# Two cross-attention heads stay on chip and their output share moves forward in a hybrid decoder trunk

## The chip, the cores and the metric

The kernel runs as one program on one core of a Trainium2 chip. The metric is the device time of one execution in microseconds (us), as the median of several runs. TensorE (PE) multiplies matrices; VectorE (DVE), ScalarE (ACT) and GpSimd (POOL) work on elements; SyncE (SP) issues the transfers between DRAM and on-chip memory.

## What is computed

One inference step of a trunk of two layers, for a prompt of 512 tokens and a sample group of 8 times 4 tokens that share all weights; both lie side by side as 544 columns. Layer 0 is a dilated attention. Layer 1, where all of the change lies, is an RWKV-7 layer with 12 heads of 64 and four heads of cross attention into 256 memory tokens. Cut to what matters (`p` is the input projection of the normalised `x`; the cross heads are the last 256 of the 1024 branch columns):

```python
y, S = wkv_scan(r, decay, k, v, -kk, kk * a, s0)
y = group_norm(y) * ln_w + ln_b + jnp.sum(r * k * r_k, axis=-1, keepdims=True) * v
o_mem = cross_attn(q_mem, mem_kv)
h = jnp.concatenate([y, o_mem], axis=-1) * jax.nn.silu(gate)
x = x + rms_norm(h @ w_out, norm_post)
```

## The kernel before

Everything is in float32. A float32 product is made on PE as three products of a high and a low part (lines 313, 314 and 315 in `mm1`: high by high, low weight by high, high weight by low input). Weights come by DMA as pieces of 128 x 512 and are split by ACT (line 305) and POOL (line 306).

Layer 1 works on rows of 128 features. There are 29 feature columns of the input projection (`column`: r, k, v and the low-rank inputs; `gate`: gates 0 to 7 and the two query columns of the cross heads), each of 8 x 2 x 3 matmuls of 272 columns. Six pairs of heads make three groups of four heads, g = 0, 1, 2. For each group there are, in this order: elementwise work on DVE (decay, keys, receptance, values), score matrices (`sc`, masked into SA and SR on DVE at line 1381), a triangular solve of 30 steps on DVE (two instructions for each step, lines 1450 and 1452, in tile T; TX is its transpose, line 1460), products on PE (X at line 1466, then w, q, v), and a recurrence over eight chunks (`recur`): PE makes z from the state St, DVE adds it to UV (line 1676), PE makes z from UV, DVE makes the next St (line 1694), and y goes to a group norm (`norm`, `normed`: sums, square on ACT, power on POOL line 1537, product yc on DVE line 1538, transposition gn on PE line 1547, and back into bv on DVE line 1558).

What sets the order: `Flow` runs Python generators, each with a rank, and picks at each step the ready one of lowest rank. A `yield a, b` books `a` us of PE work and makes the generator ready `b` us later; the table `LAT` holds such delays, `RANK` the ranks, and a dense generator (projection columns, gates, output) is let in when the `debt` of the others is over `DEBT`. So PE's order, and with it that of the other engines, is written out before the program runs. The dense generators fill PE between the dependent steps of the solve and the recurrence. `GORDER` is the order of the eight gate columns, and the first `GEARLY` of them may come before the last feature column.

The output projection is `outer`. A gate column leaves `u` = gate times (for gates 6 and 7) the cross heads' output `om`; `u` is written to DRAM (`ud`, line 1195). `gated(j)` reads it back (`ug`, line 1758), for heads 0 to 5 multiplies it with the group norm's `bv` (DVE, line 1762), and makes its high part `h` on ACT (line 1763) and its low part on POOL, or on DVE for the `j` in `LOD` (line 1764). The output has eight row tiles `mt` in two parts of the columns: part 0 is 256 wide and part 1 288. Three shares are summed in `z`: `o1b` (the cross heads 6 and 7; 16 tiles of 6 matmuls, copied to z by ACT, line 1866), `o1a` (heads 0 to 3; 16 tiles of 12 matmuls, added by DVE, line 1881), and, in `last`, `o2` (heads 4 and 5, weights w2h and w2l; added by DVE, line 1812). `o1b` waits for gates, for the end of group 1's recurrence (`end1`) and for two of its norms, since z lies in tiles (tags AR and BK) that group 1 has used.

`last(i)` then takes the squares of part i (ACT line 1815, summed on POOL line 1818 and by PE products with ones), their inverse root (`rstd_begin`, `rstd_mid`, `rstd_end`; power on POOL, line 341), and `finish` scales each row (DVE, line 1782), adds the residual (`xr`; POOL line 1788, or DVE line 1785 for the rows in `RADD`) and sends it out.

## Time and profile before

| | |
|---|---|
| median of 3 runs | 808.15 us (806.22 to 809.14) |
| the profiled execution | 807.1 us, span 805.3 us |
| PE busy | 746.5 us (93%) |
| DVE busy | 468.2 us (58%) |
| ACT, POOL busy | 340.9 us (42%), 351.9 us (44%) |
| the chain that ended last | PE 75%, DVE 12%, DMA 4%, POOL 3%, ACT 2% |
| mean granted clock of PE | 0.979 of full speed |

Times in the rows are microseconds from the start of the span. An engine's idle time in brackets stands before the instruction that ended it, with the instruction that it waited for. The granted clock is 1.00 at 2.4 GHz and 0.50 at 1.2 GHz. Tile names are the program's, without their numbers.

### The profile page before, as it was taken

To read this page: it belongs to the slowest core of one execution; us is meant where nothing else is said; L and a number is where in the kernel's file an instruction comes from. 1 tells how busy PE (TensorE), PEld (TensorE's weight loads), DVE (VectorE), ACT (ScalarE), POOL (GpSimd) and SP (SyncE) were. 2 spreads that over 40 slices of the span, in tenths; PEclk is the share of its full clock that TensorE was granted. 3 is DMA by queue.
4 is the path that set the end of the run, shared out by engine and by line. 5 is a ranking of instruction groups with operands and counts; after the bars stand their busy time and mean duration, and the time that the engine had idled before them with its cause. 6 is when DMAs were issued, how large, how long until landed. Compare 5 with 4: busy or idle time off the path is not lost.

```text
span 805.3 us, 20097 instructions
## 1 busy us (share of the span) xinstructions
PE 746.5 (93%) x8264; PEld 633.0 (79%) x8264; DVE 468.2 (58%) x1100; ACT 340.9 (42%) x787; POOL 351.9 (44%) x391
## 2 busy tenths in 40 slices
PE   6899999999988988989999999999999999799793
PEld 5777778889875776688988889898788988589673
DVE  7743312255467455663454579854699536983465
ACT  6455321134343345535786247432365332442031
POOL 3642223333220262964543347644365445463257
PEclk9999999999999999999999999999999999799996
DMA  7474398852213574325213442200222233442013
GB/s 247 124 239 141 101 285 298 279 209 82 81 54 94 212 226 144 109 89 178 68 65 93 144 148 73 74 28 28 70 70 95 81 110 98 127 129 64 31 39 111
DMA packets 59088, 99.51 MB, mean 124 GB/s; under 512 B 6415, under 2 KB 24111, under 8 KB 58959
## 3 DMA queue, kind: packets, MB, share of 16 engines
q1 hardware_dynamic: 58996, 98.22, 37.1%
q8 instruction: 65, 1.06, 0.5%
q14 instruction: 27, 0.22, 0.1%
HBM read 84.15 MB, written 14.05 MB: 122 GB/s over the span
## 4 chain that ended last, share of the span: by engine, by line
PE 75%; DVE 12%; DMA 4%; POOL 3%; ACT 2%; issue 2%; SPq 1%; POOLq 0%; ACTq 0%; DVEq 0%
PE o L313 2%; PE b_h L313 2%; PE b_h L314 2%; PE b_h L315 2%; PE o L315 2%; PE sc L1373 2%; PE o L314 2%; PE y L1636 2%; PE Sx L560 2%; PE o L777 1%; PE z L1636 1%; DMA raw_wo<-in_w_out_a 1%; PE ssz L987 1%; PE ox L584 1%; PE pa L769 1%
## 5 line engine op out<-in xcount | busy, mean ns | idle before, releaser
L306 POOL TENSOR_TENSOR lo_b<-raw_b,hi_b 128x512 fp32r<-128x512 f32 x58 | 76.6, 1320 | 117.3 <-ACT hi_b L305 83.7
L306 POOL TENSOR_TENSOR lo_a<-raw_a,hi_a 128x512 fp32r<-128x512 f32 x44 | 57.1, 1299 | 138.6 <-ACT hi_a L305 138.0
L305 ACT CAST hi_a<-raw_a 128x512 fp32r<-128x512 f32 x44 | 27.3, 620 | 67.8 <-DMA raw_a<-in_w_in_a 9.7
L305 ACT CAST hi_b<-raw_b 128x512 fp32r<-128x512 f32 x58 | 36.3, 626 | 41.8 <-PE b_h L315 14.1
L313 PE MATMUL b_h<-xg,hi_b 128*128 128x272 f32 x160 | 46.5, 299 | 0.6 <-DVE xv L1133 0.3
L314 PE MATMUL b_h<-xg,lo_b 128*128 128x272 f32 x160 | 45.9, 294 | 0.0
L315 PE MATMUL b_h<-xg,hi_b 128*128 128x272 f32 x160 | 45.4, 292 | 0.0
L1450 DVE TENSOR_TENSOR TX<-T,TT 128x30 f32<-128x30 f32 (+14 forms) x90 | 29.3, 326 | 5.8 <-ACT T L1424 4.1
L313 PEld LDWEIGHTS b_h<-xg,hi_b 128*128 128x128 f32 x160 | 29.6, 188 | 2.9 <-issue 1.8
L1452 DVE TENSOR_TENSOR T<-T,TX 128x30 f32<-128x30 f32 (+14 forms) x90 | 30.1, 334 | 2.3 <-DVE TX L1450 0.4
L314 PEld LDWEIGHTS b_h<-xg,lo_b 128*128 128x128 f32 x160 | 29.7, 188 | 0.3
L315 PEld LDWEIGHTS b_h<-xg,hi_b 128*128 128x128 f32 x160 | 29.7, 188 | 0.3 <-issue 0.2
L1678 POOL TENSOR_TENSOR Sd<-St,DF 128x128 f32<-128x128 f32 x21 | 8.4, 401 | 37.4 <-DVE St L1694 26.7
L754 ACT ACTIVATE P<-P,m 128x768 f32<-128x768 f32 x16 | 14.9, 935 | 16.3 <-DVE m L753 16.3
L1373 PE MATMUL sc<-AR,BK 64*64 64x128 f32 x384 | 19.0, 279 | 0.2 <-DVE bv L1319 0.2
L313 PE MATMUL o<-h,hi_o1a 128*128 128x256 f32 (+1 forms) x64 | 18.8, 299 | 0.0
L314 PE MATMUL o<-h,lo_o1a 128*128 128x256 f32 (+1 forms) x64 | 18.5, 291 | 0.0
L315 PE MATMUL o<-h,hi_o1a 128*128 128x256 f32 (+1 forms) x64 | 18.1, 290 | 0.0
L769 PE MATMUL pa<-ident,P 128*128 128x128 f32 x96 | 14.2, 279 | 3.6 <-DVE P L756 1.4
L769 PEld LDWEIGHTS pa<-ident,P 128*128 128x128 f32 x96 | 10.6, 142 | 6.7 <-issue 2.3
L306 POOL TENSOR_TENSOR lo_o1a<-raw_o1a,hi_o1a 128x512 fp32r<-128x512 f32 x8 | 10.6, 1325 | 11.8 <-ACT hi_o1a L305 11.8
L1282 POOL TENSOR_TENSOR rv<-rv,mhalf 128x10 f32<-128x10 f32 x6 | 14.0, 2334 | 3.7 <-DVE rv L1281 3.7
(1057 smaller groups left out, 2825.9 us busy)
## 6 DMA issues: line engine op xcount, KB each, us to landing
raw_b<-in_w_in_b SPq DMA_DIRECT2D x58, 256.0 KB, 2.6
raw_a<-in_w_in_a SPq DMA_DIRECT2D x44, 256.0 KB, 2.7
kc<-in_kc SPq DMA_DIRECT2D x18, 512.0 KB, 5.2
vc<-in_vc SPq DMA_DIRECT2D x18, 512.0 KB, 6.2
out_win<-t SPq DMA_DIRECT2D x12, 272.0 KB, 2.3
PB<-bd SPq DMA_DIRECT2D x4, 576.0 KB, 6.7
x<-in_x SPq DMA_DIRECT2D x8, 272.0 KB, 6.0
xr<-in_x SPq DMA_DIRECT2D x16, 136.0 KB, 4.3
```

Source lines behind the costliest of these rows:

```text
L305: nc.scalar.copy(hi, raw)
L306: lo_eng.tensor_tensor(lo, raw, hi.bitcast(F32), ALU.subtract)
L313: nc.tensor.matmul(ps[:, :n], hi, xh, start=first, stop=False)
L314: nc.tensor.matmul(ps[:, :n], lo, xh, start=False, stop=False)
L315: nc.tensor.matmul(ps[:, :n], hi, xl, start=False, stop=last)
L560: nc.tensor.matmul(S[hh][64 * e:64 * e + 64, 0:256], qm[r, f, a:a + 64], kT[l][r, f, :], start=True, stop=True)
L754: nc.scalar.activation(P, P, AF.Exp, bias=m1[:, 0:1], scale=1.0, accum_out=m1[:, 1:2])
L769: nc.tensor.transpose(dst, P[:, j * 128:j * 128 + 128], ident)
L1373: nc.tensor.matmul(pts[e][unit(c, j, h)[0], a:a + 128], BK[H2[h], j, x, CH[c]], AR[H2[h], j, :, CH[c]], start=True, stop=True)
L1450: nc.vector.tensor_tensor(pd, TP[:, 0:s, s:s + 1].to_broadcast([128, s, w]), TT[:, s:s + 1, s + 1:32].to_broadcast([128, s, w]), ALU.mult)
L1452: nc.vector.tensor_tensor(TP[:, 0:s, s + 1:32], TP[:, 0:s, s + 1:32], pd, ALU.add)
L1636: nc.tensor.matmul(out, lhs, rhs, start=start, stop=stop)
```

## The change

Gates 6 and 7 no longer go through DRAM. When such a gate's half is made, its high part is copied by ACT and its low part subtracted (DVE for 6, POOL for 7) into tiles `hx` that take four of the six `tmp` buffers. For those buffers the gate waits until the last group's values are made (`values5`). A new generator `crossed` makes the sixteen `o1b` tiles right behind the last gate column. Its z rows lie in five column tiles, two `tmp` tiles and one row of the later squares' tile, so only the last row waits for `end1`. `outer` begins with the `o1a` share. The squares get tiles of their own. In the last part the residual adds are dealt out anew: DVE takes rows 6 and 7 of part 0 and rows 2 and 7 of part 1, POOL the other twelve. The first three adds of part 0 stand behind the squares' sums, two more rows of part 0 are scaled ahead of `rstd_begin`, and POOL's order there is fixed by hand as DVE's was. Seven constants of the planner are new.

```diff
-GORDER = (6, 2, 5, 4, 0, 1, 7, 3)
+GORDER = (4, 0, 5, 7, 2, 6, 3, 1)
-RADD = (0,)
+RADD = (6, 7), (2, 7)
+MID = 2
-GEARLY = 2
-LAT = [4.0, 5.82, 0.81, 0.26, 5.42, 5.2, 1.5, 0.94, 1.83, 0.6, 0.87]
-RANK = [3.5, 2, 4, 3, 2, 2.5, 2.5, 9]
-RHO, DEBT = 0.35, 0.5
-LOD = (1, 3)
+GEARLY = 5
+LAT = [4.0, 4.95, 0.81, 0.26, 5.42, 2.6, 1.5, 0.9, 1.56, 0.61, 1.28]
+RANK = [5, 7, 7, 3, 2, 2.5, 2.5, 9]
+RHO, DEBT = 0.35, 0.54
+LOD = (6, 0, 2)
...
             if j >= 6:
                 nc.vector.tensor_tensor(s, s, oj[:, HALF[h]], ALU.mult)
+                nc.scalar.copy(hx[j][0][:, HALF[h]], s)
+                (nc.vector if j in LOD else nc.gpsimd).tensor_tensor(hx[j][1][:, HALF[h]], s, hx[j][0][:, HALF[h]].bitcast(F32), ALU.subtract)
+        if 6 <= j < 8:
+            hx[j] = [pp.tile([128, NT], F32R, tag="tmp", bufs=TMPB, name=f"h{j}{k}") for k in range(2)]
...
-        if j < 8:
+        if j < 6:
             nc.sync.dma_start(ud[j], uj)
+        elif j < 8 and len(hx) == 2:
+            flow.done("hx", 1.5)
...
+            if j in (6, 7):
+                yield "values5"
             yield from gate(j)
...
+        for kt in range(len(FIN)):
+            residual(0, kt, out.xr)
+        for _ in range(MID):
+            finish(0, rp0, left.pop(0), out.xr, False)
         rv = rstd_begin(acc, n, "p11", 4e-6)
...
+    def crossed():
+        yield "columns"
+        yield "hx"
+        zt = [col(f"z1{mt}") for mt in range(5)]
+        zt += [tmp(f"z1{mt}") for mt in (5, 6)]
+        for mt in range(8):
+            if mt == 7:
+                yield "end1"
+                out.sq = [rw.tile([128, 2176], F32, tag=("AR", "BK")[i], bufs=2, name=f"sq1{i}") for i in range(2)]
+                zt.append(out.sq[0][:, 0:NT])
...
     def outer():
         yield "gates"
         out.h1 = pxg.tile([128, 2, 8, NT], F32R, tag="xg", name="h1")
-        for j in (6, 7):
-            gated(j)
-            yield 0.0, 1.0
-        for e in ("end1", "norm1_8", "norm1s"):
+        yield "crossed"
+        for e in ("norm1_8", "norm1s"):
             yield e
-        out.z = [by_row(i, ("AR", "BK")[i], 2176, "z1")[1] for i in range(2)]
+        for m in range(4):
+            gated(m)
...
+    flow.spawn(9.5, crossed(), True)
```

**Where the instructions go.** Up to about 400 us every engine's order is the same. PE's matmuls are the same in number and shape over the whole program, and also over the stretch up to the first `o1a` tile.

On PE, where the output share begins: in the kernel before the last gate column ends some rows earlier, transposes of the last group (`bk5s`) stand before it, and the first two tiles o000 and o001 (row tile 0, parts 0 and 1) interleave their halves for heads 6 and 7.

```order
L1362 MATMUL bk5s_8511<-ident_75,BK2_7065 32x64 x4
L313 MATMUL o000_9546<-h1_9492,hi_o1b0_9537 128x256
L314 MATMUL o000_9546<-h1_9492,lo_o1b0_9538 128x256
L313 MATMUL o001_9585<-h1_9492,hi_o1b0_9537 128x288
L314 MATMUL o001_9585<-h1_9492,lo_o1b0_9538 128x288
L315 MATMUL o000_9546<-h1_9492,hi_o1b0_9537 128x256
L315 MATMUL o001_9585<-h1_9492,hi_o1b0_9537 128x288
L313 MATMUL o000_9546<-h1_9492,hi_o1b0_9537 128x256
L314 MATMUL o000_9546<-h1_9492,lo_o1b0_9538 128x256
L313 MATMUL o001_9585<-h1_9492,hi_o1b0_9537 128x288
L314 MATMUL o001_9585<-h1_9492,lo_o1b0_9538 128x288
L315 MATMUL o000_9546<-h1_9492,hi_o1b0_9537 128x256
```

In the changed kernel the last gate column (`b11`) stands directly before the tiles, and the operands are `h60` to `h71`, made by the gates themselves.

```order
L314 MATMUL b11_h1_9222<-xg1_3424,hi_b11_1_9217 128x272
L315 MATMUL b11_h1_9222<-xg1_3424,lo_b11_1_9218 128x272
L316 MATMUL b11_h1_9222<-xg1_3424,hi_b11_1_9217 128x272
L314 MATMUL o000_9532<-h60_8811,hi_o1b0_9528 128x256
L315 MATMUL o000_9532<-h60_8811,lo_o1b0_9529 128x256
L316 MATMUL o000_9532<-h61_8812,hi_o1b0_9528 128x256
L314 MATMUL o000_9532<-h70_8618,hi_o1b0_9528 128x256
L315 MATMUL o000_9532<-h70_8618,lo_o1b0_9529 128x256
L316 MATMUL o000_9532<-h71_8619,hi_o1b0_9528 128x256
L314 MATMUL o001_9542<-h60_8811,hi_o1b0_9528 128x288
```

What moved: the 16 tiles are the same 96 matmuls, now behind 43 matmuls of gate columns (before 17) since the end of group 1's recurrence, and without the tile `h1` that was read back from DRAM.

On PE, in the recurrence of the last group (z2 and y2, with its states St2_0 to St2_7): before, tiles of the heads' share (o170, o171) stand between the steps, 50 matmuls between the first z and the fourth step.

```order
L315 MATMUL o170_10037<-h1_9492,hi_o1a7_10033 128x256
L313 MATMUL o170_10037<-h1_9492,hi_o1a7_10033 128x256
L314 MATMUL o170_10037<-h1_9492,lo_o1a7_10034 128x256
L315 MATMUL o170_10037<-h1_9492,hi_o1a7_10033 128x256
L1636 MATMUL z2_9188<-St2_2_9308,AR2_7064 64x64 x4
L1636 MATMUL y2_0_9228<-St2_1_9267,AR2_7064 64x64 x2
L1636 MATMUL y2_0_9228<-St2_2_9308,AR2_7064 64x64 x2
L313 MATMUL o171_10051<-h1_9492,hi_o1a7_10033 128x288
L314 MATMUL o171_10051<-h1_9492,lo_o1a7_10034 128x288
```

In the changed kernel nothing but the sample group's small products stands between the steps.

```order
L1645 MATMUL z2_9164<-St2_1_9259,AR2_6998 64x64 x4
L1645 MATMUL y2_0_9204<-UV2_7477,SR2_7476 64x64 x8
L1645 MATMUL y2_0_9204<-St2_0_9173,AR2_6998 64x64 x2
L1645 MATMUL y2_0_9204<-UV2_7477,SR2_7476 64x64 x8
L1645 MATMUL z2_9164<-UV2_7477,BK2_6999 64x64 x8
L1645 MATMUL z2_9164<-St2_2_9300,AR2_6998 64x64 x4
L1645 MATMUL y2_0_9204<-St2_1_9259,AR2_6998 64x64 x2
L1645 MATMUL y2_0_9204<-St2_2_9300,AR2_6998 64x64 x2
L1645 MATMUL z2_9164<-UV2_7477,BK2_6999 64x64 x8
L1645 MATMUL z2_9164<-St2_3_9344,AR2_6998 64x64 x4
```

What moved: the heads' share. Twelve of its 16 tiles stand ahead of the last group's first solve product X, six before; the other four stand between X and w, and none is left behind w. Ten of DVE's adds for these tiles then stand ahead of the transposition TX, four before. In the same way, the transposition norm `gn` of the last chunks (gn2_6) stands behind the first two `o2` tiles; before it stood behind the first four.

On POOL, at the end of the program (L1818/L1840 squares, L1788/L1808 residual adds, rv_p11 the power of part 1): before, two adds of part 0 stand among the squares and twelve adds behind the power.

```order
L1818 TENSOR_TENSOR sqo101_10194<-sqo101_10194,sqo141_10243 128x288
L1788 TENSOR_TENSOR z10_9530<-z10_9530,xr10_10065 128x256
L1818 TENSOR_TENSOR sqo101_10194<-sqo101_10194,sqo151_10254 128x288
L1788 TENSOR_TENSOR z10_9530<-z10_9530,xr10_10065 128x256
L341 TENSOR_TENSOR rv_p11_10292<-rv_p11_10292,mhalf_80 128x3
L1788 TENSOR_TENSOR z10_9530<-z10_9530,xr10_10065 128x256 x5
L1788 TENSOR_TENSOR z11_9531<-z11_9531,xr11_10175 128x288 x6
L1788 TENSOR_TENSOR z17_9532<-z17_9532,xr17_10176 128x288
```

In the changed kernel three stand behind the squares and nine behind the power: three of part 0 and six of part 1.

```order
L1840 TENSOR_TENSOR sq11_9745<-sq11_9745 128x288 x5
L1808 TENSOR_TENSOR z10_9519<-z10_9519,xr10_10073 128x256
L1808 TENSOR_TENSOR z11_9520<-z11_9520,xr10_10073 128x256
L1808 TENSOR_TENSOR z12_9521<-z12_9521,xr10_10073 128x256
L342 TENSOR_TENSOR rv_p11_10286<-rv_p11_10286,mhalf_80 128x3
L1808 TENSOR_TENSOR z13_9522<-z13_9522,xr10_10073 128x256
L1808 TENSOR_TENSOR z14_9523<-z14_9523,xr10_10073 128x256
L1808 TENSOR_TENSOR z15_9524<-z15_9524,xr10_10073 128x256
L1808 TENSOR_TENSOR z10_9519<-z10_9519,xr11_10175 128x288
L1808 TENSOR_TENSOR z11_9520<-z11_9520,xr11_10175 128x288
```

What moved: three adds from POOL's end to earlier places or to DVE.

On DVE, two places of the earlier groups differ. Ahead of the transposition TX of group 0 one product xr (line 1308), four masked copies SA and SR (line 1381) and two sums bv (line 1319) are added, and one product of a gate (line 1192) is gone, while PE has less work ahead of that group's X: 32 more score matmuls of 128 columns, 19 fewer column matmuls. And the transposition TT of the next group's scores (line 1418) stands elsewhere in the recurrences: in that of group 0 it stood behind the norm's yc, and now stands ahead of it; in that of group 1 it stood behind the last UV add, and now stands ahead of a UV add in the middle and of yc.

## Rows read from the trace of the kernel before

Rows of windows give the stretch, its length, the busy time (and number of instructions) of PE, PEld, DVE, ACT and POOL, then the granted clock of PE, the DMA share and GB/s.

**Rows 1.** Windows, 620 to 713 us, across the end of the gate columns
```profile
620.00:680.00 60.00, 60.00 (x1145) 54.00 (x1137) 35.34 (x81) 15.89 (x34) 27.25 (x29) 1.00 0.29 92
680.00:690.00 10.00, 8.14 (x104) 6.47 (x98) 6.84 (x23) 5.75 (x13) 4.78 (x8) 0.98 0.35 97
690.00:699.00 9.00, 6.54 (x24) 5.21 (x26) 8.61 (x19) 3.34 (x8) 4.21 (x3) 0.50 0.46 145
699.00:713.00 14.00, 12.37 (x111) 10.14 (x108) 12.44 (x34) 7.31 (x19) 7.19 (x8) 0.97 0.42 124
```

**Rows 2.** Timeline of PE, 684 to 692 us: start, duration, instruction [idle before <-releaser]
```profile
684.03 0.63 PE L1636 MATMUL y<-UV,SR 64*64 64x64 f32 x16
...
688.61 0.51 PE L315 MATMUL o<-h,hi_o1b 128*128 128x256 f32 x2 [0.67 <-POOL h L1764]
691.96 0.58 PE L313 MATMUL o<-h,hi_o1b 128*128 128x256 f32 x1 [2.84 <-ACT h L1763]
```

**Rows 3.** Timeline of ACT, 691 us
```profile
691.26 0.65 ACT L1763 CAST h<-ug 128x544 fp32r<-128x544 f32 x1 [2.50 <-DMA ug<-ud]
```

**Rows 4.** Timeline of PE, two tiles of the output projection further on
```profile
714.70 0.29 PE L313 MATMUL o<-h,hi_o1a 128*128 128x288 f32 x1
...
717.71 0.30 PE L313 MATMUL o<-h,hi_o1a 128*128 128x288 f32 x1
```

**Rows 5.** Timeline of DVE, 693 us
```profile
693.83 0.68 DVE L1538 TENSOR_TENSOR yc<-yc,gst 128x512 f32<-128x512 f32 x1
```

**Rows 6.** Timeline of PE, first solve product of group 0
```profile
513.90 1.01 PE L1466 MATMUL X<-TX,SA 32*32 32x32 f32 x52 [1.47 <-DVE TX L1460]
```

**Rows 7.** Timeline of DVE, 497 to 515 us
```profile
497.74 0.77 DVE L1308 SCALAR_TENSOR_TENSOR xr<-xr,pv,kf 128x544 f32<-128x544 f32 x1
...
508.56 1.55 DVE L1192 TENSOR_TENSOR u<-u,om 128x272 f32<-128x272 f32 x1
...
514.05 0.42 DVE L1319 TENSOR_TENSOR bv<-bo,xv 128x272 f32<-128x272 f32 x1
514.39 0.41 DVE L1192 TENSOR_TENSOR u<-u,om 128x272 f32<-128x272 f32 x1
```

**Rows 8.** Waits of PE, 400 to 806 us: total, times, longest
```profile
PE gn L1547 <- DVE yc L1538: 3.2, 3, 1.8
...
PE o L313 <- DVE z L1812: 1.9, 4, 0.8
...
PE b17h L313 <- DVE xr L1141: 1.1, 1, 1.1
```

**Rows 9.** Timeline of DVE, 566 us
```profile
565.92 2.17 DVE L1418 STREAM_TRANSPOSE TT<-SA 128x1024 f32<-128x1024 f32 x1
```

**Rows 10.** Timeline of PE, the last group's recurrence, 755 to 760 us
```profile
755.33 0.34 PE L1636 MATMUL z<-St,AR 64*64 64x64 f32 x8 [0.48 <-DVE St L1694]
...
760.21 0.34 PE L1636 MATMUL z<-St,AR 64*64 64x64 f32 x8 [1.01 <-DVE St L1694]
```

**Rows 11.** Timeline of POOL, 765 to 768 us
```profile
765.07 1.21 POOL L1594 TENSOR_TENSOR UX<-UVs,smask 128x512 f32<-128x512 f32 x1 [3.04 <-DVE gst L1535]
...
767.30 1.01 POOL L1537 TENSOR_TENSOR gst<-gst,mhalf 128x4 f32<-128x4 f32 x1
```

**Rows 12.** Groups of instructions, 785 to 806 us: busy us, mean ns | idle before
```profile
L1788 POOL TENSOR_TENSOR z<-z,xr 128x288 f32<-128x288 f32 x7 | 5.3, 783 | 0.0
L1788 POOL TENSOR_TENSOR z<-z,xr 128x256 f32<-128x256 f32 x7 | 5.1, 754 | 0.0
...
L1785 DVE TENSOR_TENSOR z<-z,xr 128x288 f32<-128x288 f32 x1 | 0.9, 876 | 0.0
...
L1785 DVE TENSOR_TENSOR z<-z,xr 128x256 f32<-128x256 f32 x1 | 0.5, 480 | 0.0
```

**Rows 13.** Windows, 742 to 784 us, columns as in the first group
```profile
742.00:764.00 22.00, 18.12 (x415) 15.91 (x411) 9.88 (x27) 2.26 (x6) 7.01 (x10) 1.00 0.16 49
764.00:784.00 20.00, 17.89 (x178) 13.46 (x178) 13.34 (x39) 5.86 (x15) 11.33 (x15) 0.91 0.12 39
```

More of the change, by code (lines that the diff above doesn't have):

```diff
@@ L1740, in dense, with values5 @@
         flow.done("columns")
+    def values5():
+        yield from values(5)
+        flow.done("values5")
     def gates():
@@ L1830, in last @@
             return
+        for kt in range(len(FIN)):
+            residual(0, kt, out.xr)
+        for _ in range(MID):
+            finish(0, rp0, left.pop(0), out.xr, False)
         rv = rstd_begin(acc, n, "p11", 4e-6)
         turn()
+        turn(G, "lastp")
         rvx = rstd_mid(rv, n, "p11")
@@ L1835, in last @@
         while left:
-            finish(0, rp0, left.pop(0), out.xr)
+            finish(0, rp0, left.pop(0), out.xr, False)
+        for kt in range(len(FIN), 8):
+            residual(0, kt, out.xr)
         rp = rstd_end(rvx, n, zs[:, 512:1024])
```

54 lines of the change are left out of this document (31 added, 23 removed).

## The prediction

> **What bounds the kernel now.** I read the windows first, then PE's waits, then the timelines around the places that the order moves. From 620 to 680 us PE is busy for all 60.00 us [rows 1]: there nothing is won except by doing less, and the change does the same matmuls. Behind the gate columns this ends. Between 680 and 713 us PE is busy for 8.14 of 10, 6.54 of 9 and 12.37 of 14 us, so 5.95 us idle, and from 690 to 699 us its granted clock is 0.50, the lower level of 1.2 GHz [rows 1]. The reader should see why in the timeline: after the first four matmuls of the cross heads' share PE waits 0.67 us for POOL's low part and 2.84 us for ACT's high part [rows 2], and that ACT copy itself stood 2.50 us waiting for ug, the gated output on its way back from DRAM [rows 3]. So in this stretch PE is the bound, and a read from DRAM ends last.
>
> The time lost there is the first term. Idle 5.95 us; 6.54 us of work at 0.50 would take half at full clock, so 3.3 us; the windows at 0.98 and 0.97 give 0.16 and 0.37 us more, together 0.5. That makes 9.7 us.
>
> **The change, part by part.** All terms are differences in PE's lost time, since PE's matmuls stay the same. They are added to the profiled execution, 807.1 us (its span of 805.3 us and 1.8 us around it), and then to the median of the runs shown, 808.15 us, which stands 1.05 us above it.
>
> *1. The output share behind the last gate.* The round trip through DRAM is gone, so the 9.7 us go, but new waits come. The norm gn of group 1's last chunks still stands among the tiles. Before, from the end of y (684.03 and 0.63, so 684.66 us) to the end of DVE's yc (694.51) there are 9.9 us [rows 2, 5]. Now PE has for this time 21 column matmuls and 36 of the share. Twelve matmuls of 288 and twelve of 256 columns take 717.71 less 714.70, 3.01 us, 0.125 each [rows 4], so 57 take 7.1 us and 2.8 us are left over. No row shows how much DVE's chain shortens without the read of ug in its queue; I allow up to 1.5 us. So 1.3 to 2.8 us, I take 2.3, nearer to the long end because solve steps stand in between as before. The tiles have two PSUM buffers, and ACT, which empties them, now also has two h copies of 0.65 us [rows 3] in its queue that wait for DVE: 0 to 1.4 us, I take 0.7. Together -9.7 + 2.3 + 0.7 = **-6.7 us** (-8.4 to -5.5).
>
> The new high and low parts of heads 6 and 7 (two halves each) lie between gate columns while PE is full; their cover is that stretch's column work, and without it each would cost about the 0.65 us of such a copy [rows 3]. The waits for `values5` and `hx` stand in generators and only set the order; their effect is in the places below. SP loses four transfers of ud and ug, and none of the others gets later by it.
>
> *2. The earlier groups, rearranged.* PE waits 1.47 us for DVE before X of group 0 [rows 6]. Ahead of it DVE now has one product of 0.77 us, four masked copies and two sums more. A sum starts 0.34 us before the next row (514.05, 514.39), and a copy is about as wide, so that is 0.77 + 6 x 0.34 = 2.8 us; one gate product goes, which took 1.55 us at one place and 0.34 at another [rows 7]. DVE is 1.3 to 2.5 us later. PE comes earlier: 19 column matmuls less are 2.4 us, 32 score matmuls of 128 columns more are 1.9 us by their width at most and half of it if two run side by side, so 0.5 to 1.4 us. The wait grows by 1.8 to 3.9 us, and by as little as 0.5 if DVE has slack that I don't see. I take 2.6, the middle of what DVE and PE give without it. In group 0's recurrence gn's wait of 1.8 us [rows 8] gets more matmuls ahead of it, but DVE's transposition of 2.17 us [rows 9] now stands before yc and a UV add: -1.8 to +1.2, I take -0.6. In group 1's the same transposition stands in mid-recurrence: 0 to 2.2, I take 1.5, since the steps wait for exactly these adds. The wait of 1.1 us of a gate column for xr [rows 8] goes, as another column stands there. Sum 2.6 - 0.6 + 1.5 - 1.1 = **+2.4 us** (-2.4 to +6.2).
>
> *3. From the heads' share to the last group's recurrence.* Six more tiles stand ahead of X: 72 matmuls, 9.0 us [rows 4]. That is work moved, not added, but X comes 9.0 - 6.7 = 2.3 us later on PE, and DVE has six more adds of about 0.42 us (by a sum of like width [rows 7]) ahead of TX, 2.5 us: X waits 0.2 us. What is lost is cover. Where nothing fills the recurrence a step idles 0.48 to 1.01 us [rows 10]; three more steps are now bare, though two of them hold the sample's products. 0 to 3.0 us, I take 0.8. Sum **+1.0 us** (0 to +5.0 with X waiting 2.2).
>
> *4. The turn to the last two parts.* The norm gn of chunks 4 and 5 now stands ahead of two tiles, and its power on POOL (1.01 us) stands behind UX (1.21 us) [rows 11] and two low parts, so it is late. In exchange PE's waits for DVE's adds of `o2`, four with 1.9 us together [rows 8], shrink, since the tiles stand closer to the end of the recurrence. From -1.9 to +3.0 us, the whole of the one to UX, power and a low part in a row; I take **+0.8**, a little above the middle.
>
> *5. The end.* Behind the last power POOL has nine residual adds, before twelve. Two of 754 ns and one of 783 ns [rows 12] go, 2.3 us; I take **-1.9**, since DVE's added rows delay its scaling a little (-2.3 to 0).
>
> Sum: -6.7 + 2.4 + 1.0 + 0.8 - 1.9 = -4.4 us, so 802.7 us for an execution like the profiled one and **803.7 us** for the median.
>
> **Rule and row.** DVE's two adds of this kind took 876 ns (288 wide, among POOL's adds) and 480 ns (256 wide), POOL's took 783 and 754 [rows 12]: one of DVE's two was slowed by about 0.35 us, POOL's were not. The Trainium skill, page "SBUF — State Buffer", section "Who interferes with whom", says that a DVE instruction with two SBUF inputs and a GpSimd instruction that reads SBUF exclude each other for a whole instruction. By that rule each of the two adds of part 1 on DVE would hold POOL up for about 0.45 us, term 5 would be about -1.0 and the sum 804.6 us. The slowed row agrees with it, the 480 ns row does not, so the sum keeps -1.9; 804.6 lies in the forecast's own range and shares its chance.
>
> **The rivals.**
>
> *No change that can be measured.* DVE becomes the bound: it is busy 8.61 of 9 us in the middle of the old stall [rows 1], and the change gives it work before two solves. If X of group 0 waits 3.9 more, group 1 gives 2.2, gn of group 1 its full 2.8, ACT's buffers 1.4 and step 4 another 0.6 us, the sum is worse by 1.3 + 0.7 + 0.5 + 0.7 + 0.6 = 3.8: 807.5 us. For it speaks that the solve is a chain on DVE and can't be spread.
>
> *A larger gain.* The bounds at the low side: X of group 0 at 0.5 (2.1 better), group 1 at 0 (1.5), gn and buffers at 1.3 and 0 (1.7), so 5.3 better: 798.4 us. For it speaks that PE waited only where a row names one late producer, and that column work can slide into small gaps.
>
> *Slower: the clock falls in the bare recurrence.* From 742 to 764 us PE was busy 18.12 of 22 us at clock 1.00; from 764 to 784 us 17.89 of 20 at 0.91 [rows 13]. Now 6.2 us of tiles (50 matmuls [rows 4]) leave the first stretch, so 12 us of work in about 16 remain, in small pieces with gaps. If the clock goes to 0.50 there and stays so until the last part, each microsecond of full-clock work costs one more; with 9 us of work affected the sum is 812.7 us. It decides from 8.5 us on. Against it: the bare steps before kept 1.00 [rows 10, 13], and the fall to 0.50 came after a wait of 2.84 us [rows 2]. The Trainium skill, page "TensorE: Matmul & The Clock Gate", section "A second HAM failure mode: psum-queue depth-cycling", tells of a kernel whose frequent small gaps between groups of matmuls made the clock swing. The rows of the bare steps do not show this so far.
>
> That the change doesn't do what it says is excluded: the order shows the tiles directly behind the last gate column, with operands that never left the chip.
>
> **How the numbers follow.** About 0.5%, 4.0 us, is what a measurement of this kernel can tell from no change: faster is below 804.1, slower above 812.2 us. The forecast (801.5 to 806) has 0.48; it lies just beyond the bound, so 0.30 of it counts as faster. No measurable change has 0.24, of which 0.02 reach over 812.2; the larger gain 0.18; the clock 0.10. So faster 0.30 + 0.18 = 0.48, same 0.18 + 0.22 = 0.40, slower 0.10 + 0.02 = 0.12. The range of 797 to 810 us takes in the first three cases with their bounds and leaves the clock's out.
>
> **What would show it.** Right: between group 1's end and the heads' tiles no wait of PE for a DMA, a clock near 1.00 and under 4 us idle; a longer wait before group 0's X; gaps of 0.5 to 1 us in the last recurrence; nine adds behind the last power. Wrong: a wait for ACT or DVE of over 3 us among the sixteen tiles, X of the last group waiting over 2 us, or a clock of 0.50 behind 735 us for longer than 4 us.

## The result, and the profile after

The changed kernel took 802.06 us (median of 6 runs, 798.51 to 805.44) against 807.9 us for the kernel before (6 runs, 803.99 to 810.96): a ratio of 0.991, 95% interval 0.9886 to 0.9935. The forecast of 803.7 us was 1.6 us too high. The profiled execution of the change had a span of 796.7 us and is the fastest of its six, so the two profiles differ by 8.6 us where the medians differ by 5.8.

The first reading is the place of term 1, in windows of the changed kernel over the same kind of stretch as [rows 1], with the same columns:

```profile
618.00:678.00 60.00, 59.17 (x1109) 51.17 (x1108) 33.95 (x77) 18.90 (x43) 26.93 (x30) 1.00 0.26 81
678.00:688.00 10.00, 9.43 (x103) 9.01 (x103) 8.42 (x27) 4.69 (x11) 3.36 (x3) 1.00 0.47 149
688.00:697.00 9.00, 8.08 (x67) 7.10 (x67) 8.79 (x22) 5.89 (x14) 7.20 (x6) 1.00 0.57 154
697.00:711.00 14.00, 13.36 (x111) 12.95 (x110) 11.99 (x31) 5.98 (x14) 8.90 (x9) 1.00 0.56 160
```

Where PE had been busy for 8.14 of 10, 6.54 of 9 and 12.37 of 14 us, it is now busy for 9.43, 8.08 and 13.36, and the granted clock is 1.00 throughout, before 0.50 in the middle window [rows 1]. No DMA ends a wait here any more. What is left are three waits for ACT, which empties the two PSUM buffers. PE's timeline among the first of the sixteen tiles, and the norm gn that I had priced at 2.3 us:

```profile
684.74 0.28 PE L314 MATMUL o<-h,hi_o1b 128*128 128x256 f32 x1
...
686.17 0.40 PE L314 MATMUL o<-h,hi_o1b 128*128 128x288 f32 x1 [0.57 <-ACT z L1894]
...
690.45 0.63 PE L1556 MATMUL gn<-ident,yc 128*128 128x128 f32 x4
```

The norm gn of group 1's last chunks stands at 690.45 without a wait. The waits of PE from 400 us to the end answer to [rows 8]:

```profile
PE z L1645 <- DVE St L1703: 3.0, 4, 1.5
PE o L314 <- ACT z L1894: 2.1, 3, 0.9
PE gn L1556 <- DVE yc L1547: 2.1, 3, 1.7
PE ssz L356 <- ACT rvx_p L349: 1.8, 1, 1.8
...
PE z L1645 <- DVE UV L1685: 1.0, 2, 0.8
PE sc L1382 <- DVE BK L1307: 0.9, 1, 0.9
...
PE o L314 <- DVE z L1833: 0.8, 2, 0.5
PE gn0s L1559 <- DVE yc0s L1547: 0.7, 1, 0.7
```

X of group 0, which had waited 1.47 us for DVE [rows 6] and for which I forecast 2.6 us more, is not in this list: it waits for nothing. Other waits for DVE stand ahead of it now, of `sc` for BK (0.9 us) and of `bo` for tw (0.5 us).

To see the whole, I cut both profiles at the same events. Both are counted from a common landmark ahead of all changed code, the transposition `rs_x` (at 351.74 us before and 353.70 after: the work ahead of it, in the same order in both kernels, took 2.0 us longer in the profiled execution of the change). In each stretch two kinds of loss are summed over windows of 1 us: **idle** is length less PE's busy time, **half clock** is busy time times (1 - granted clock).

| stretch | before: length, idle / half clock | after: length, idle / half clock |
|---|---|---|
| `rs_x` to X of group 0 | 162.2, 3.4 / 0.0 | 161.3, 3.1 / 0.0 |
| to X of group 1 | 111.2, 5.0 / 1.7 | 108.0, 2.3 / 0.0 |
| to the end of group 1's recurrence | 55.0, 0.0 / 0.0 | 54.9, 0.8 / 0.0 |
| to the first `o1a` tile | 33.1, 5.9 / 3.7 | 24.1, 2.1 / 0.0 |
| to X of group 2 | 9.2, 0.0 / 0.0 | 18.2, 0.0 / 0.0 |
| to the first `w2h` tile | 43.7, 4.3 / 0.8 | 33.9, 4.3 / 1.6 |
| to the second part's first tile | 14.9, 1.4 / 0.9 | 19.3, 4.2 / 1.9 |
| to the end | 24.3, 12.8 / 0.8 | 23.5, 12.3 / 1.7 |
| sum | 453.6, 32.8 / 7.9 | 443.0, 29.1 / 5.2 |

The lengths of single stretches also hold work that has moved between them; the losses don't. From the landmark on the change gains 10.6 us: 6.4 of it are less loss (40.7 to 34.3), the rest, 4.2 us, is less **work**, which here means length less both losses. For the same matmuls I had counted that as nothing; part of the modelled ends of matmuls may be in it. Of the 10.6 us the 2.0 ahead of the landmark go off: 8.6.

These are single executions. Later runs have the same order of PE in large parts, and their profiles tell which of the differences come back (`tail_only` has the order of the kernel before; `no_tail`, `radd_pool`, `hold2`, `hold4` and `fill` have that of the change up to the end of group 1's recurrence):

| | order before: before, `tail_only` | order of the change |
|---|---|---|
| loss, end of group 1's recurrence to the first `o1a` tile | 9.6, 9.2 | 2.0 to 2.3 in all six |
| idle, `rs_x` to the end of group 1's recurrence | 8.4, 8.7 | 5.3 to 7.4 in all six |
| half clock, `rs_x` to the end of group 1's recurrence | 1.7, 0.0 | 0.0 twice, 1.6, 6.8 three times |
| loss, from the landmark to the end | 40.7, 37.3 | 34.3, `no_tail` 37.4, `radd_pool` 41.9 |
| work, from the landmark to the end | 412.9, 413.0 | 408.7, `no_tail` 408.6, `radd_pool` 407.2 |

So the gain behind the last gate comes back each time, and so does the smaller amount of work in the three kernels listed. In the earlier groups only the idle part does; the half clock there comes and goes with the execution, so that the full 3.9 us by which this profile loses less there (10.1 and 6.2) is not shown to belong to the change. On the mean of the last two rows the losses fall by 1.1 us and the work by 4.8, together 5.9, as much as the medians differ.

At the end term 5 is not to be seen: 12.8 and 0.8 against 12.3 and 1.7. The groups of the residual additions after 783 us answer to [rows 12]:

```profile
L1808 POOL TENSOR_TENSOR z<-z,xr 128x288 f32<-128x288 f32 x6 | 4.8, 822 | 0.8 <-DVE z L1797 0.8
L1808 POOL TENSOR_TENSOR z<-z,xr 128x256 f32<-128x256 f32 x6 | 4.6, 787 | 0.0
L1805 DVE TENSOR_TENSOR z<-z,xr 128x288 f32<-128x288 f32 x1 | 1.1, 1087 | 0.0
L1805 DVE TENSOR_TENSOR sq<-sq,xr 128x256 f32<-128x256 f32 x1 | 0.9, 946 | 0.0
L1805 DVE TENSOR_TENSOR sq<-sq,xr 128x288 f32<-128x288 f32 x1 | 0.9, 945 | 0.0
L1805 DVE TENSOR_TENSOR z<-z,xr 128x256 f32<-128x256 f32 x1 | 0.8, 806 | 0.0
```

All four of DVE's additions are now as slow as only one of its two was [rows 12], GpSimd's are 33 and 39 ns longer than before, and one of GpSimd's waits 0.8 us for DVE.

So the removed round trip was worth a little more than forecast; the earlier groups, where I had forecast a loss, gave some 1 to 3 us of idle time, in this profile 3.9 with the clock; and there is less work, which I had not forecast at all. The experiments ask where these come from, and whether each part pays alone.

### The profile page after: what moved, and what is told of

It is laid out like the page before. It is cut to its first block, busy times and chain, and to the rows that moved or that the text cites. A ratio compares the mean times of both kernels' runs of the same rounds, so it can differ in the third digit from the quotient of the medians.

```text
span 796.7 us, 20090 instructions
## 1 busy us (share of the span) xinstructions
PE 743.2 (93%) x8264; PEld 633.3 (79%) x8264; DVE 463.0 (58%) x1104; ACT 341.0 (43%) x789; POOL 351.8 (44%) x389
## 4 chain that ended last, share of the span: by engine, by line
PE 71%; DVE 13%; POOL 5%; DMA 4%; ACT 3%; issue 3%; SPq 0%; POOLq 0%; DVEq 0%; ACTq 0%
PE o L314 2%; PE b_h L314 2%; PE o L315 2%; PE o L316 2%; PE b_h L316 2%; PE b_h L315 2%; PE o L778 2%; PE Sx L561 2%; PE sc L1382 1%; PE ssz L988 1%; PE ox L585 1%; PE z L1645 1%; PE pa L770 1%; PE y L1645 1%; PE ptx L577 1%
## 5 line engine op out<-in xcount | busy, mean ns | idle before, releaser
L755 ACT ACTIVATE P<-P,m 128x768 f32<-128x768 f32 x16 | 14.9, 935 | 16.3 <-DVE m L754 16.3
L316 PE MATMUL o<-h,hi_o1a 128*128 128x256 f32 (+1 forms) x64 | 18.2, 286 | 0.0
L1382 PE MATMUL sc<-AR,BK 64*64 64x128 f32 x384 | 16.8, 276 | 1.1 <-DVE BK L1307 0.9
L1703 DVE TENSOR_TENSOR St<-z,Sd 128x128 f32<-128x128 f32 x21 | 6.0, 288 | 18.7 <-PE z L1645 12.8
L770 PEld LDWEIGHTS pa<-ident,P 128*128 128x128 f32 x96 | 10.6, 142 | 6.7 <-issue 2.3
```

Source lines behind the costliest of these rows:

```text
L316: nc.tensor.matmul(ps[:, :n], hi, xl, start=False, stop=last)
L770: nc.tensor.transpose(dst, P[:, j * 128:j * 128 + 128], ident)
L1382: nc.tensor.matmul(pts[e][unit(c, j, h)[0], a:a + 128], BK[H2[h], j, x, CH[c]], AR[H2[h], j, :, CH[c]], start=True, stop=True)
```

## The experiments

The runs were made in three lots, each beside its own runs of the kernel before (808.45, 808.07 and 808.06 us); each kernel was run 6 to 12 times. The landmarks and losses of all of them are worked out as above.

**The last part's order alone** (`tail_only`), and **the change without it** (`no_tail`). The edit of the first, on the kernel before:

```
-RADD = (0,)
+RADD = (6, 7), (2, 7)
+MID = 2
```

with `turn`, `finish`, `residual` and the end of `last` as in the change; the second is the reverse edit on the changed kernel.

> The kernel before with only the last part's new order (residual adds dealt out anew, two rows scaled ahead of the root, POOL's order fixed). If three adds fewer behind the last power shorten the end, as term 5 of the prediction has it: 1.9 us less, ratio 0.9976. If DVE's and POOL's adds exclude each other, as the changed kernel's profile suggests (DVE's adds 0.81 to 1.09 us beside POOL's): 0 to 1 us less, ratio 0.999 to 1.000, and DVE's adds on line 1785's successor over 0.8 us.

> The changed kernel with the last part as before. If the end is worth 1.9 us: ratio to before 0.9935. If it is worth nothing: 0.991, as the changed kernel. The rest of the profile as in the changed kernel: no wait of PE for a DMA in the output share.

`tail_only` took 807.91 us, ratio 0.9994 (0.9969 to 1.002); `no_tail` 802.74 us, ratio 0.9928 (0.9899 to 0.9957), against the change's 0.991. The last part's order is worth nothing that can be measured. GpSimd's timeline at the end of `tail_only` shows the same as in the change:

```profile
795.27 0.86 POOL L342 TENSOR_TENSOR rv_p<-rv_p,mhalf 128x3 f32<-128x3 f32 x1 [0.25 <-DVE rv_p L341]
796.09 3.96 POOL L1794 TENSOR_TENSOR z<-z,xr 128x256 f32<-128x256 f32 x5
800.87 3.25 POOL L1794 TENSOR_TENSOR z<-z,xr 128x288 f32<-128x288 f32 x4 [0.82 <-DVE z L1783]
```

Nine additions take 7.2 us and the wait for DVE 0.82, 8.0 in all. In the kernel before, twelve stood there:

```profile
793.80 8.90 POOL L1788 TENSOR_TENSOR z<-z,xr 128x256 f32<-128x256 f32 x12
```

That is 0.9 us less, and the end comes 3.0 us behind the last addition (3.2 in the change) where it came 2.6 behind it. So 0.3 to 0.5 remain of the 1.9.

**The constants of the planner, apart from the structure.** `old_table` is the changed kernel with all the old constants, `new_table` the kernel before with all the new ones:

```
-GORDER = (4, 0, 5, 7, 2, 6, 3, 1)
-GEARLY = 5
-LAT = [4.0, 4.95, 0.81, 0.26, 5.42, 2.6, 1.5, 0.9, 1.56, 0.61, 1.28]
-RANK = [5, 7, 7, 3, 2, 2.5, 2.5, 9]
-RHO, DEBT = 0.35, 0.54
-LOD = (6, 0, 2)
+GORDER = (6, 2, 5, 4, 0, 1, 7, 3)
+GEARLY = 2
+LAT = [4.0, 5.82, 0.81, 0.26, 5.42, 5.2, 1.5, 0.94, 1.83, 0.6, 0.87]
+RANK = [3.5, 2, 4, 3, 2, 2.5, 2.5, 9]
+RHO, DEBT = 0.35, 0.5
+LOD = (1, 3)
```

> The changed kernel with all the planner's old constants (GORDER, GEARLY, LAT, RANK, DEBT, LOD): heads 6 and 7 stay on chip and the share follows the last gate column, but the order of the earlier groups is made by the old table. If the gain is the round trip through DRAM that is gone (theory 1): it stays, 5 to 7 us less, ratio 0.992 or below. If it is the planner's table (theory 2), which lost 4 us less before the end of group 1's recurrence: ratio 0.996 to 1.000, and waits before that point come back (X of group 0 over 1 us).

> The kernel before with all the new constants, but heads 6 and 7 still through DRAM. Theory 1: the wait for ug stays or grows, ratio 0.998 to 1.005, and a stretch at clock 0.50 behind it. Theory 2: 4 us less before the end of group 1's recurrence, ratio 0.995, with the wait for ug still there.

`old_table`: 813.15 us, ratio 1.0086 (1.0052 to 1.0121). `new_table`: 809.46 us, ratio 1.0014 (0.9991 to 1.0038). For `new_table` that is theory 1; for `old_table` neither expectation allowed a slower kernel. **Neither half of the change gains anything alone.** The losses by stretch (idle / half clock) say why:

| stretch | after | `old_table` | `new_table` |
|---|---|---|---|
| `rs_x` to the end of group 1's recurrence | 6.2 / 0.0 | 8.5 / 4.4 | 5.7 / 3.4 |
| to the first `o1a` tile | 2.1 / 0.0 | 1.7 / 0.0 | 7.4 / 5.5 |
| to the first `w2h` tile | 4.3 / 1.6 | 6.0 / 9.3 | 5.3 / 0.0 |

With the new constants in the old structure group 1's recurrence ends 2.3 us sooner after the landmark (326.06 against 328.33), and the stretch of the round trip then loses 12.9 us instead of 9.6: what comes early waits. PE's waits in `new_table` from 678 to 712 us:

```profile
PE o L313 <- ACT z L1866: 2.3, 2, 1.9
PE o L313 <- ACT h L1763: 1.5, 1, 1.5
PE gn L1547 <- DVE yc L1538: 1.5, 1, 1.5
```

With the old constants in the new structure the round trip's loss is gone as well (1.7), but more is lost in the earlier groups (12.9, where the kernel before lost 10.1) and above all in the last recurrence. Windows of `old_table`, 728 to 772 us:

```profile
728.00:750.00 22.00, 20.46 (x413) 19.26 (x411) 12.96 (x26) 4.03 (x8) 5.10 (x6) 0.92 0.10 26
750.00:772.00 22.00, 18.01 (x384) 15.14 (x382) 8.48 (x24) 2.31 (x7) 7.07 (x10) 0.65 0.16 49
```

A clock of 0.65 over 22 us: the slower rival of the prediction, which the change escaped. This execution took 816.97 us, 3.8 above the median of its kernel, so that its 9.3 us may be more than the usual loss.

**Which constants?** I first suspected the old gate order. It begins with gate 6, which in the changed code waits for the event `values5`, the last group's values, and so it holds back the gates behind it. `old_costs` keeps the new gate order and sets only LAT, RANK and DEBT back; `fit_table` sets everything back, but with the gates in the order (4, 2, 5, 6, 0, 1, 7, 3); `old_rank` sets back one line:

```
-RANK = [5, 7, 7, 3, 2, 2.5, 2.5, 9]
+RANK = [3.5, 2, 4, 3, 2, 2.5, 2.5, 9]
```

> The changed kernel with the planner's old LAT, RANK and DEBT; its gate order, GEARLY and LOD stay. The old table as a whole gave 1.009 of before, but its gate order begins with gate 6, which in the new structure must wait for group 2's values, and it held back every gate: none lay under group 0's inversion. Theory 1 (that gate order alone spoiled the old table; the removed round trip pays with any costs): 803 to 806, ratio 0.993 to 0.997, lost time from the end of group 1's recurrence to the first o1a about 2, and 11 or less from o1a to w2h. Theory 2 (the planner's costs and ranks carry half of the gain, by the order of the recurrences' matmuls): 808 to 813, with over 10 lost up to the end of group 1's recurrence or over 10 from o1a to w2h.

> The changed kernel with all of the planner's old constants, but the gate order 4 2 5 6 0 1 7 3 in place of 6 2 5 4 0 1 7 3 (gates 4 and 6 change places), so that no gate waits for group 2's values before others can go. Theory 1: X of group 0 no later than before against the common landmark (162, before 162.2) where the old table as it was had 161.2, but X of group 1 at 273 to 274 (276.5 with the old table), and 804 to 807. Theory 2 (the costs and ranks carry it): 809 to 813, as with the old table as it was. Together with the run of the old costs it tells the gate order from the costs.

> The changed kernel with the old RANK alone (decay 3.5, keys and values 2, scores 4, in place of 5, 7, 7: small steps of the next group go before the dense columns and gates); LAT and DEBT stay new. With the old LAT, RANK and DEBT together it was 818. Theory 1 (the ranks put the small dependent steps at once into PE's queue, where it waits for them): 812 to 820, X of group 1 near 276 after the common landmark. Theory 2 (the latencies that the planner reckons with do it, keys' 5.2 for 2.6 above all): 800 to 806, X of group 1 at 269 to 272.

`old_costs`: 817.97 us, ratio 1.0122 (1.0083 to 1.0162). `fit_table`: 817.8 us, 1.0104 (1.0069 to 1.014). `old_rank`: 820.58 us, 1.0157 (1.0119 to 1.0195). My suspicion fell: with the gates in a workable order the time is no better. The first two came out above even the second theory's range (up to 813). The ranks alone do it, and more than all constants together; 820.58 lies just above the range of theory 1. In `old_rank` X of group 0 comes a little sooner (159.9 after the landmark, after 161.3), X of group 1 13.4 us later (282.7 against 269.3), later than I had expected. The stretch between the two X is 14.8 us longer (122.8 and 108.0), of which 6.8 are loss (9.1 and 2.3) and 8.0 are work that stands ahead of X of group 1 instead of behind it: the trace counts 192 matmuls of gates there, where the change has 151. Work that has gone ahead can't cover what comes behind: between the first `o1a` tile and X of group 2 `old_rank` loses 12.2 us, the change nothing. PE's waits of `old_rank` over its two bad stretches, 515 to 635 us and 705 to 734 us:

```profile
PE kn L1286 <- ACT BK L1281: 2.8, 1, 2.8
PE b_h L314 <- DVE xv L1134: 1.9, 1, 1.9
...
PE gn1s L1559 <- DVE yc1s L1547: 3.0, 1, 3.0
PE sts L1608 <- DVE bv L1567: 1.3, 1, 1.3
PE o L314 <- ACT h L1778: 1.2, 1, 1.2
```

and its window of 706 to 733 us:

```profile
706.00:733.00 27.00, 18.78 (x154) 15.42 (x153) 25.30 (x70) 5.59 (x11) 10.79 (x10) 0.81 0.42 122
```

beside the same place of the change, 702 to 720 us:

```profile
702.00:720.00 18.00, 18.00 (x145) 17.89 (x143) 15.14 (x41) 5.25 (x9) 9.06 (x7) 1.00 0.46 131
```

There DVE is busy for 25.30 of 27 us and PE for 18.78: DVE's work has piled up where group 2's solve needs DVE. The old ranks put `keys`, `values` and `scores` (2, 2, 4) ahead of dense work; each such step stands in PE's queue as soon as the planner thinks it ready, and where its operand is late (`kn` by 2.8 us, a column for `xv` by 1.9) everything behind it waits. From the landmark on `old_rank` is 19.5 us longer than the change: 5.8 are idle (34.9 and 29.1), 9.9 half clock (15.1 and 5.2) and 3.8 work. So half of the price was paid through the clock, whose mean over an execution was 0.956 to 0.970 in the six runs of `old_rank` and 0.971 to 0.985 in those of the change. That the ranks are the cause is shown; that the waits in PE's queue bring the lower clock with them is not, and which of the three numbers does it was not tried.

**Work dealt into the last recurrence.** Term 3 had priced its bare steps. `hold2` and `hold4` take the last two and four of the sixteen `o1a` tiles out of the dense stream and put them, six matmuls at a time, between the recurrence's half steps:

```
+            if g == 2:
+                pull()
             for k in (1, 0):
                 for j, h in PAIRS:
...
+            if g == 2:
+                pull()
```

where `pull` takes the next six matmuls of the tiles kept back and fixes their place in PE's order among the recurrence's own. The last recurrence also begins only when the planner has placed the other tiles.

> The changed kernel with the last two of the 16 tiles of the heads' first share taken out of the stretch around X of group 2 and dealt by hand, six matmuls at a time, into the first steps of the last recurrence. Theory A (PE and VectorE are both bound where X of group 2 starts, 720: the tiles move from a place where they cost 2.7 us to one where they fill gaps of 0.5 us each): X of group 2 waits for the transposed TX by up to 2.7 us, the recurrence's first steps take up to 1.5 us longer, end within 1.5 us of the changed kernel: 800 to 803.5. Theory B (the recurrence without filling costs through the half clock, 1.5 us and more): 2 to 4 us faster than the changed kernel, granted clock over 0.9 in 750 to 780. Theory C (the steps are behind the tiles: each block delays the recurrence by its full 0.69 us): 2 to 3 us slower, 804 to 805.

> The same with the last four tiles (eight blocks of six matmuls, one in each half step of the first four steps). Theory A: X of group 2 waits about 2 to 4 us, the gaps take most of the blocks: 800 to 804. Theory B: 3 to 5 us faster than the changed kernel. Theory C: 4 to 6 us slower, 806 to 808.

`hold2`: 803.18 us, ratio 0.9931 (0.9907 to 0.9955). `hold4`: 800.03 us, 0.989 (0.9856 to 0.9924). Neither can be told from the change, 0.991 (0.9886 to 0.9935), and B's 3 to 5 us don't come: theory A, with a smaller wait than it allowed. From X of group 2 to the end `hold4` takes 77.4 us, the change 76.7, and one more tile (1.5 us by [rows 4]) lies behind that X. X of group 2 waits 0.3 us. So the bare steps cost about what their cover is worth elsewhere. The sums show where the gain of the cover goes: behind the first `o1a` tile `hold4` loses 22.8 us where the change loses 26.0, but its work there, for 1143 matmuls in each, is 71.8 us against 68.9 (`hold2` 70.3; before 71.1). So the same matmuls take longer where tiles and small steps alternate. That would account for about half of the smaller amount of work in the change, the 2 us behind that tile; the other half, ahead of it, stays open.

**Fillers.** Is it the clock that the bare recurrence costs? `fill` adds matmuls to the change that compute nothing that is used, `fill_old` adds the same to `old_table`:

```
+        def fill(m):
+            for _ in range(m if g == 2 else 0):
+                put(pf[:, 0:128], ident, ident, True, True)
...
+            fill(2)
             for k in (1, 0):
...
+            fill(2)
```

> The changed kernel with matmuls that compute nothing (the identity by itself, 128 columns, into a tile that nobody reads), two behind each half step of the last recurrence. Theory A (the gaps of that recurrence cost little through the clock: 1.6 us of the changed kernel's loss between X of group 2 and the first w2h tile lay at half clock, 4.3 were idle): the fillers put 0.2 to 0.5 us into each half step where no gap is left, 802 to 806. Theory B (the half clock there and in the tiles behind it, 1.6 + 1.9, is what the bare recurrence costs): time at half clock between X of group 2 and the second part's tiles below 0.5 us and 800 or less.

> The same fillers in the kernel with all of the old constants (813.15, with 9.3 us lost at half clock and 5.2 idle between X of group 2 and the first w2h tile). Theory A (there the clock falls for want of work on PE): the half-clock loss of that stretch falls below 2 us and the kernel comes to 804 to 808. Theory B (it falls with the small matmuls themselves, filled or not): over 6 us at half clock stay, 812 to 816.

`fill`: 804.49 us, ratio 0.9961 (0.9938 to 0.9983). The window of `fill` from X of group 2 on, to be read beside the change's from 720 to 754 us below it:

```profile
723.50:762.50 39.00, 37.13 (x825) 32.25 (x824) 17.71 (x41) 6.33 (x14) 12.33 (x17) 1.00 0.12 36
```

```profile
720.00:754.00 34.00, 29.70 (x770) 25.96 (x769) 16.95 (x38) 5.92 (x14) 10.98 (x15) 0.95 0.12 36
```

The clock is 1.00 now, idle time falls from 4.3 to 1.9 us, and up to the second part's tiles 0.1 us of half clock is left, which is B's first mark. But the stretch is 5 us longer and the time is A's. `fill_old`: 814.05 us, 1.0081 (1.0048 to 1.0114), no better than `old_table`. There the half-clock loss of that stretch falls from 9.3 to 3.3 us, between the two expectations (below 2, over 6), and the stretch still takes 40.4 us after 38.6. So with matmuls in the gaps less of that stretch runs at the lower clock, which speaks for A. The same holds over all runs: span times (1 - granted clock) has a mean of 25.9 us in `old_table` and 18.6 in `fill_old`, 7 us less. But the time doesn't fall: the added matmuls cost as much as they save, and A's 804 to 808 us don't come.

**All residual additions on GpSimd** (`radd_pool`):

```
-RADD = (6, 7), (2, 7)
+RADD = (), ()
```

> The changed kernel with all residual additions of the last part on GpSimd (RADD empty): 13 behind the power of the second part's root in place of 9, and none on VectorE. In the changed kernel VectorE's four additions took 0.81 to 1.09 us beside GpSimd's, which took 0.80 each with a wait of 0.82 for VectorE; in the kernel before twelve of GpSimd's took 0.74 each. Theory A (two engines that add at the same time hinder each other, so that the split pays little): GpSimd's additions 0.74 to 0.76 each, 9.7 us in all against 8.0, the time within 2 us of the changed kernel: 802 to 804. Theory B (the split pays its full price of 0.78 for each addition moved): 3 us slower, 805.

800.4 us, ratio 0.9905 (0.9869 to 0.9941): again not to be told from the change. GpSimd's timeline at its end:

```profile
787.97 0.86 POOL L342 TENSOR_TENSOR rv_p<-rv_p,mhalf 128x3 f32<-128x3 f32 x1 [0.39 <-DVE rv_p L341]
788.80 2.77 POOL L1808 TENSOR_TENSOR z<-z,xr 128x256 f32<-128x256 f32 x4
791.53 0.72 POOL L1808 TENSOR_TENSOR sq<-sq,xr 128x256 f32<-128x256 f32 x1
792.21 5.28 POOL L1808 TENSOR_TENSOR z<-z,xr 128x288 f32<-128x288 f32 x7
797.45 0.79 POOL L1808 TENSOR_TENSOR sq<-sq,xr 128x288 f32<-128x288 f32 x1
```

Thirteen additions without a wait take 9.4 us, 0.73 each; the change's nine take 8.0 with the wait. From the power to the end there are 13.1 us against 12.0: four additions moved are worth 1.1 us and not four times 0.78. That is theory A's mechanism; its time of 802 to 804 us was put too high.

## Why the prediction was right, and where its terms were not

The sign, the size and the range held, but terms on both sides of the sum were wrong, and their errors partly cancelled. The first term, the largest, held in mechanism and in size and came back in every profile of this order; the third held in loss. The premise of the sum, that all terms are differences in PE's lost time, failed too: the work, taken as equal, fell by 4.2 us, as much as the whole forecast of 4.4. By the losses in the two profiles:

1. **The share behind the last gate: -6.7 forecast, -7.5 measured** (9.6 to 2.1). The reading of the profile was right: a wait for a DMA, a copy behind it, and work at half clock in its wake. Within it the price of gn, 2.3 us, was wrong: from the end of y to the end of yc DVE takes 8.2 us (before 9.9), since 8 steps of the solve stand in it and not 14, PE has work for just as long, and gn waits for nothing. Instead ACT's emptying of the PSUM buffers cost 2.1 us in three waits where I had 0.7.

2. **The earlier groups: +2.4 forecast, -3.9 in these two profiles** (10.1 to 6.2 up to the end of group 1's recurrence), of which 2.2 are idle time and 1.7 half clock; only the idle part comes back in the other profiles. This is the step that failed. Its largest part was X of group 0, +2.6: I added up the lengths of the instructions that DVE gets ahead of X. DVE was to be 1.3 to 2.5 us later and PE 0.5 to 1.4 us earlier. Instead DVE's way from the first step of group 0's solve to the transposition ahead of X took 39.3 us, 1.0 us less than before. Windows of DVE's way, the change first, then the kernel before:

```profile
473.41:512.74 39.33, 37.70 (x334) 35.39 (x333) 36.59 (x104) 26.54 (x62) 24.42 (x26) 1.00 0.25 75
```

```profile
471.55:511.92 40.37, 39.92 (x332) 37.58 (x327) 36.04 (x98) 27.57 (x64) 24.55 (x26) 1.00 0.27 83
```

DVE is busy for 0.55 us more (36.59 and 36.04) and idle for 1.6 us less (2.7 and 4.3): before, it waited in the solve for PE (`xa`, 0.9 us) and ACT (`xk`, 0.7 and 0.3), the slack that the prediction did not see. And PE comes to X 0.6 us later and not earlier (161.25 us after the landmark; before, without its wait, 160.69), having waited elsewhere. So X's own wait of 1.5 us went to nothing, but up to X PE idles for nearly as long as before (3.1 and 3.4 us). In five of the six profiles of this order DVE's way takes 39.3 us; in `no_tail` it takes 41.1, and there too X doesn't wait for DVE.

That DVE's busy time grew by only 0.55 us has to do with lengths. The number of instructions was right and the lengths were not. First the change, then the kernel before:

```profile
504.72 0.72 DVE L1308 SCALAR_TENSOR_TENSOR AR<-tw,AR 128x544 f32<-128x544 f32 x1
...
510.08 0.42 DVE L1193 SCALAR_TENSOR_TENSOR u<-gt,b_h 128x272 f32<-128x272 f32 x1
...
512.74 1.98 DVE L1469 STREAM_TRANSPOSE TX<-T 128x1024 f32<-128x1024 f32 x1
```

```profile
505.49 1.89 DVE L1299 SCALAR_TENSOR_TENSOR AR<-tw,AR 128x544 f32<-128x544 f32 x1
```

The same product took 0.72 us instead of 1.89. What ran beside it, and beside the gate product of 1.55 us at 508.56 [rows 7], stands in GpSimd's timeline of the kernel before:

```profile
505.03 1.76 POOL L1256 TENSOR_TENSOR AR<-BK,tw 128x544 f32<-128x544 f32 x1 [1.23 <-DVE BK L1255]
...
508.52 1.29 POOL L306 TENSOR_TENSOR lo_b<-raw_b,hi_b 128x512 fp32r<-128x512 f32 x1
```

GpSimd's two end at 506.79 and 509.81. DVE's, which began 0.46 and 0.04 us behind them, end at 507.38 and 510.11, so 0.59 and 0.30 us later, which is about what each needs by itself (0.72 and some 0.34). So DVE seems to have stood until GpSimd was done. The rule of the Trainium skill ("SBUF — State Buffer", "Who interferes with whom") that the prediction weighed for term 5 would have served here better than there: the order before held some 2.4 us of standing still ahead of TX, of which the prediction had the gate product's 1.2 as one of two prices, and the new order has other neighbours. In the change, where DVE's product began 0.10 us ahead of GpSimd's next, it took 0.72; two other products of this width, 1.01 and 0.99 us long, seem to stand still for some 0.3 us each. No run sets GpSimd's order alone.

The rest of the term: gn's wait of 1.8 us in group 0's recurrence [rows 8] shrank to 0.3, where I had taken 0.6 off; the wait of 1.1 us for xr went, as forecast; group 1's recurrence, for which I had 1.5 more, lost 0.8. The 2.6 was called the middle of 1.8 and 3.9, which is 2.85.

3. **The last recurrence: +1.0 forecast, +0.8 measured** (5.1 to 5.9, with the stretch ahead of X of group 2; 7.3 in `no_tail` and `radd_pool`). Right in loss, but not the whole account: the same matmuls take less time when they stand together, and `hold2` and `hold4` show that filling the recurrence again gives nothing back. (Its upper bound of 5.0 should be 3.0 + 2.2, so 5.2.)

4. **The turn to the last parts: +0.8 forecast, +3.8 in the profile** (2.3 to 6.1), 1.0 of it at half clock. `no_tail` and `radd_pool` lose 3.3 each there, so +1.0 may be the better figure. In this profile gn waits 1.7 us, by the cause named: the power behind UX on GpSimd; in those two it waits 0.5 at most.

5. **The end: -1.9 forecast, about -0.3 by GpSimd's additions, +0.4 by the whole stretch** (13.6 to 14.0). Mis-sized: I took the 480 ns of one row as DVE's price, the row that spoke against the rule. The rows of the change speak for it. All of DVE's additions beside GpSimd's took 806 to 1087 ns, and GpSimd's additions 787 and 822 ns on average, where without DVE's they took 726 and 792 in `radd_pool`. The Trainium skill, page "SBUF — State Buffer", section "Who interferes with whom", says that the two exclude each other for a whole instruction; all four rows of the change agree with it in direction, and the measured gain is below the -1.0 us that I had worked out by it.

The signs that the prediction named: of those for being right only the longer wait before group 0's X is missing; of those for being wrong neither a wait of over 3 us among the sixteen tiles (2.1 in all) nor one of X of the last group came. The clock was at 0.50 behind 735 us in three stretches of under 4 us each and in the last 10 us, in which PE is busy for 0.2 us (before, in the last 12.8 us, for 1.1).

The rivals. *No change* did not come, though DVE is nearly full in one window of the change (8.79 of 9 us from 688 to 697): PE's waits there are for ACT. `old_rank` shows at 706 to 733 us what a bound on DVE looks like. *Slower by the clock* did not come, but is real: `old_table` is that case, with 9.3 us at half clock in the last recurrence. It came with the old constants in the new structure; with the same constants the kernel before loses 0.8 us there. The *larger gain*, 798.4 us, lies 3.7 us below what was measured.

How far the agreement is luck: in these profiles term 2 missed by -6.3 us, terms 4 and 5 by +3.0 and +2.3, the 4.2 us less work were not forecast at all, and the medians differ by 2.8 us less than the profiles. Term 1 apart, that the sum came within 1.6 us is luck. The size of each term is known from single executions, which differ by up to 7 us among six runs of one kernel.

## What to carry to other kernels

A stall that ends in a read from DRAM was found and priced well here by reading three rows behind one another (9.7 us read, 9.6 lost before and 2.1 after). The gain from taking it out is kept only if the order around it is set anew: `old_table` gave the whole gain back around the place, and `new_table`, the new order without the new structure, gained nothing. Lengths on DVE are not properties of the instruction (0.72 and 1.89 us for one product here): where the same form has two lengths, look at what GpSimd runs beside it before adding them up, and count DVE's own waits as well. The same matmuls need not take the same time in another order. One profile of one execution does not give the size of a term: see which differences come back in other profiles of the same order. And in a program whose order a planner sets by ranks, a rank that lets small dependent steps go first is not free: one line of ranks was worth 18 us here.
